# Pieces of one stage among the steps of the next: output projection and norm of a token segment between query chunks, a selection in two halves, a load two steps early

## The chip, the cores and the metric

The kernel runs on one core of a Trainium2 chip. The metric is device time in microseconds (us) of one execution, as the median over runs. TensorE (PE) multiplies, VectorE (DVE), ScalarE (ACT) and GpSimd (POOL) work on tiles, and SyncE (SP) issues most of the transfers; POOL issues the gathers. Each of them works through its own list of instructions in order.

## The reference, cut to what matters

One layer of a trunk: token mixers with carried states, their output projection, and a mixture of single-neuron experts that are found by product keys (`peer`). The part that the change touches begins where the mixers' branch outputs have been merged:

```python
out = jnp.einsum('bld,de->ble', merged, w_out)
h = h + out
xn = rms_norm(h, norm_ffn)
qh = jnp.einsum('td,de->te', xn, w_query).reshape(T, 8, 2, 128)
s = jnp.einsum('thpd,hpnd->thpn', qh, sub_keys)
sv, si = lax.top_k(s, 16)
cand = (sv[:, :, 0, :, None] + sv[:, :, 1, None, :]).reshape(T, 8, 256)
top_s, pos = lax.top_k(cand, 16)
gate = jax.nn.softmax(top_s, axis=-1)
act = jax.nn.gelu(jnp.einsum('thkd,td->thk', expert_u[eidx], xn))
y = jnp.einsum('thk,thkd->td', gate * act, expert_v[eidx])
```

Here T is 576 tokens, D is 1024 (8 blocks of 128), there are 8 heads with two half queries each, and eidx are the indices of the 16 chosen experts.

## The kernel before, in words

Products are taken in split precision: an operand becomes a high and a low part (`split`, L131: ACT writes the high part by a copy, DVE or POOL the low part by a subtraction in L134), and three matmuls (high·high, high·low, low·high) replace one (`mm3`, L136). Names ending in h and l are such parts. The weights of a block come in by `weights` (L142): SP loads the raw block of 512 KB into one of three buffers (`wraw`), the split puts its parts into one of two buffer pairs (`whl`).

The tokens stand in two segments, `SEG`: the first done is the one with 320 columns (called the first segment below), then the one with 256 (the second). The stages around the change are these.

- `merge` (L937) merges the branches, then for each segment does the output projection in 8 chunks e: 24 matmuls into `po`, and y = x + po on DVE (L974). After a segment's 8 chunks comes its RMS norm (`norm`, L980): the squares are summed (ACT squares, POOL adds, PE sums over partitions into `rmsrow`), turned and broadcast by small matmuls (`rmscol`, `rmsbc`), DVE computes the reciprocal root (L160 to L164), then eight times xnt = y·gain·rms (L986), and its two parts: x2gh and x2gl for the first segment, x2h and x2l for the second. For the first segment there are also transposes (`xtp`) that later stages read.
- `scored` (L1059) takes the queries, again segment by segment, in 16 chunks c (head and half). A chunk has 24 matmuls into `pq`, from the weight w_q[c], a copy to `qT` on ACT, and the scores `psc` against the keys on PE, one chunk later. ACT copies the scores to `sc`, and DVE finds the top 16 of each row block (`top16`, L1044: MAX8, FIND_INDEX8, MATCH_REPLACE8, MAX8, FIND_INDEX8). Chunks of heads 0 to 3 have two row blocks in the first segment, those of heads 4 to 7 have three. A chunk of the second segment has two.
- In the first segment the low part of w_q[c] is computed, by DVE for the first four chunks and by POOL for the other twelve, and written to DRAM (`wqd`); in the second segment it is loaded from there (L1041), in the chunk that uses it, while the high part is again a copy by ACT.
- After the first segment `select` (L1152) does the selection of the token block 0 for all 8 heads: candidates, top 16 of them (`tv`, `ti`), ranks, and the sums with `eq` that turn ranks into expert indices (`gi`). The gathers of expert rows, on POOL (L1379), need gi.
- After the second segment follows the long stage with all experts (`hidden`: `uh` and `ul` are parts of the expert weights in_u, `pz` its products).

A scheduler sets the order of the instructions of each engine from the program and its own estimates; the order of the buffers ("wr", "wl", "uh" and the like) follows the program. Three lines that say how the weights rotate:

```python
raw = self.wraw.tile([P, n, P], F32, name="wr", tag="wr")          # 3 buffers, w_out and w_q alike
hi = self.whl.tile([P, n, P], F32R, name="wh", tag="wh")           # 2 buffers
self.split(wh, wl, t, nc.vector if c < 4 else nc.gpsimd)           # first segment
```

Of the kernel before, what the change touches and what calls it, by code (L numbers as in the profile page):

```python
# [9 lines left out]
F32 = mybir.dt.float32  # L10
# [12 lines left out]
P = 128  # L23
D = 1024
# [97 lines left out]
class Net:  # L122
# [801 lines left out]
    def branches(self):  # L924

        nc = self.nc
        op = self.right.enter_context(self.pool("oT", side="right"))
        self.o = oh, ol = [], []
        for c in range(KC):
            t = op.tile([P, NT], F32, name="oraw", tag="ld", bufs=4)  # L930
            nc.sync.dma_start(t, self.spo[c // H][:, c % H, NMETA:])
            oh.append(op.tile([P, NT], F32R, name=f"oh{c}"))
            ol.append(op.tile([P, NT], F32R, name=f"ol{c}"))
            self.split(oh[c], ol[c], t)


    def merge(self):  # L937

        tc, nc, I = self.tc, self.nc, self.I
        oh, ol = self.o  # L940
        with self.pool("mg") as mp, self.pool("mw", 2) as wp, \
                self.pool("mps", 4, space=PSUM) as ps, self.pool("mps2", 1, space=PSUM) as ps2, self.pool("mps3", 1, space=PSUM) as ps3:
            mh = [mp.tile([P, NT], F32R, name=f"mh{c}") for c in range(KC)]
            ml = [mp.tile([P, NT], F32R, name=f"ml{c}") for c in range(KC)]
            for d in range(KC):
                wh, wl = self.weights(I["w_br"][d])
                sg = []
                for g in range(2):
                    t = wp.tile([P, NT], F32, name=f"sg{g}", tag=f"sg{g}")
                    nc.sync.dma_start(t, self.spl[8 + 2 * g + d // H][:, d % H, NMETA:])  # L950
                    sg.append(t)
                for o, w in SEG:
                    pa = [ps.tile([P, 512], F32, name="pbr", tag="ps") for _ in range(2)]
                    for g in range(2):
                        for k in range(H):
                            self.mm3(pa[g][:, :w], wh[:, H * g + k, :], wl[:, H * g + k, :], oh[H * g + k][:, o:o + w],
                                     ol[H * g + k][:, o:o + w], k == 0, k == H - 1)
                    for g in range(2):
                        v = sg[g][:, o:o + w]
                        nc.vector.tensor_tensor(v, v, pa[g][:, :w], op=ALU.mult)  # L960
                nc.vector.tensor_add(sg[0], sg[0], sg[1])
                self.split(mh[d], ml[d], sg[0])
# [789 lines left out]
```

## Time and profile before

| what | value |
|---|---|
| median of three runs | 1930.38 us (1926.36, 1930.38, 1931.58) |
| the profiled execution's own time | 1928.89 us |
| its span | 1927.1 us |
| PE busy | 1883.9 us, 98% |
| DVE busy | 1580.1 us, 82% |
| ACT, POOL busy | 908.3 us, 705.5 us |
| output projection of the second segment | about 618 to 648 us |
| query chunks, first and second segment | about 649 to 723 us, 723 to 781 us |

Between the span and the execution's own time lie 1.8 us. The page lists busy time by engine, the chain of work that ended last, and groups of instructions; the trace can also be asked for stretches, for waits of one engine (with the instruction that ended the wait), and for a timeline. A busy PE is one that has instructions under way, also where their pace is slow. The place of a time in this document is its distance from the start of the span.

### The profile page before, as it was taken

The numbers are of one execution on the slowest core, as the hardware profiler recorded it, in microseconds if no ns is written. First come the engines' busy times: TensorE is split into PE (matmuls) and PEld (weight loads), VectorE is DVE, ScalarE is ACT, GpSimd is POOL, SyncE is SP. The second block draws the span as 40 slices with busy tenths as digits, with TensorE's granted clock in tenths as the row PEclk, the third lists the DMA queues.
The fourth block names the chain that finished last, engine by engine and source line by source line (L and its number), as shares of the span: only waits on it lengthen the run. The fifth ranks groups of instructions, "written<-read, shape, count | busy, mean of one in ns | idle before, by whom it ended". The sixth has DMA issues, their size and how long they took to land.

```text
span 1927.1 us, 31932 instructions
## 1 busy us (share of the span) xinstructions
PE 1883.9 (98%) x11759; PEld 1715.2 (89%) x11759; DVE 1580.1 (82%) x2962; ACT 908.3 (47%) x1598; POOL 705.5 (37%) x519
## 2 busy tenths in 40 slices
PE   7999999999999999999999999999999999999998
PEld 7898999888999899999999999999888788787786
DVE  5677676676465779999999998788999888988897
ACT  5542334263324555544868899533333333333333
POOL 1110010300001241244444444466667565655660
PEclk9999999999999999999999999999999999999999
DMA  7355333465554879899999999999999999999993
GB/s 253 98 162 167 96 94 108 143 191 177 186 156 155 260 268 336 292 342 336 349 353 351 394 389 388 376 385 393 402 399 401 398 400 401 400 400 401 398 401 128
DMA packets 224388, 564.86 MB, mean 293 GB/s; under 512 B 31986, under 2 KB 96242, under 8 KB 222568
## 3 DMA queue, kind: packets, MB, share of 16 engines
q1 hardware_dynamic: 168792, 361.47, 53.0%
q0 software_dynamic: 55296, 201.35, 27.2%
q8 instruction: 92, 1.51, 0.3%
q14 instruction: 64, 0.52, 0.1%
q10 hardware_dynamic: 144, 0.01, 0.0%
HBM read 483.28 MB, written 78.16 MB: 291 GB/s over the span
## 4 chain that ended last, share of the span: by engine, by line
PE 65%; DMA 20%; DVE 12%; issue 2%; ACT 1%; SPq 0%; DVEq 0%; ACTq 0%
PE pz L138 9%; PE pz L140 9%; PE pz L139 8%; PE py L1591 7%; DMA wj<-wd 7%; PE acc L138 5%; PE acc L140 5%; PE acc L139 5%; DMA wr<-in_v 4%; DMA gz<-gz 4%; PE pw L1309 2%; DVE ul L1485 2%; PE py L666 1%; PE pz L661 1%; DVE gr L1391 1%
## 5 line engine op out<-in xcount | busy, mean ns | idle before, releaser
L1379 POOL DMA_INDIRECT gr<-in_ur,gi x192 | 300.9, 1567 | 321.0 <-DVE yt L1398 206.2
L1379 POOL DMA_INDIRECT gr<-in_v,gi x192 | 303.1, 1579 | 233.9 <-DVE gr L1391 172.1
L1479 ACT ACTIVATE uh<-wr 128x1024 fp32r<-128x1024 f32 x256 | 270.0, 1056 | 204.8 <-PE py L1591 95.7
L138 PE MATMUL pz<-x2h,uh 128*128 128x384 f32 x1024 | 346.6, 338 | 0.0
L140 PE MATMUL pz<-x2h,ul 128*128 128x384 f32 x1024 | 342.7, 335 | 0.2
L139 PE MATMUL pz<-x2l,uh 128*128 128x384 f32 x1024 | 342.3, 334 | 0.0
L1485 DVE TENSOR_TENSOR ul<-wr,uh 128x1024 fp32r<-128x1024 f32 x256 | 311.9, 1218 | 9.4 <-PE pz L140 3.9
L1398 DVE SCALAR_TENSOR_TENSOR yt<-gr,ga,yt 128x1024 f32<-128x1024 f32 x192 | 245.7, 1280 | 10.0 <-DMA gr<-in_v,gi 9.1
L1391 DVE SCALAR_TENSOR_TENSOR gr<-gr,xt 128x1024 f32<-128x1024 f32 x192 | 233.6, 1218 | 12.6 <-DMA gr<-in_ur,gi 12.4
L138 PE MATMUL acc<-xnh,wh 128*128 128x296 f32 (+1 forms) x768 | 233.1, 304 | 8.1 <-ACT xnh L299 6.5
L140 PE MATMUL acc<-xnh,wl 128*128 128x296 f32 (+1 forms) x768 | 233.5, 305 | 0.2 <-DVE wl L134 0.2
L139 PE MATMUL acc<-xnl,wh 128*128 128x296 f32 (+1 forms) x768 | 233.1, 304 | 0.5 <-DVE xnl L300 0.5
L1591 PE MATMUL py<-ul,ah 128*128 128x512 f32 x768 | 201.5, 396 | 4.7 <-DVE ul L1485 4.7
L1591 PE MATMUL py<-uh,ah 128*128 128x512 f32 x768 | 201.8, 397 | 3.3 <-ACT ah L1565 2.7
L1591 PE MATMUL py<-uh,al 128*128 128x512 f32 x768 | 200.6, 395 | 0.0
L140 PEld LDWEIGHTS pz<-x2h,ul 128*128 128x128 f32 x1024 | 192.2, 188 | 0.9 <-DVE ul L1485 0.9
L138 PEld LDWEIGHTS pz<-x2h,uh 128*128 128x128 f32 x1024 | 192.3, 188 | 0.1
L139 PEld LDWEIGHTS pz<-x2l,uh 128*128 128x128 f32 x1024 | 192.4, 188 | 0.0
L133 ACT ACTIVATE wh<-wr 128x1024 fp32r<-128x1024 f32 x88 | 93.1, 1058 | 197.5 <-issue 69.0
L1591 PEld LDWEIGHTS py<-ul,ah 128*128 128x128 f32 x768 | 143.3, 188 | 42.4 <-DVE ul L1485 8.2
L1591 PEld LDWEIGHTS py<-uh,ah 128*128 128x128 f32 x768 | 143.1, 188 | 39.2 <-ACT ah L1565 4.6
L1591 PEld LDWEIGHTS py<-uh,al 128*128 128x128 f32 x768 | 144.1, 188 | 35.1
(430 smaller groups left out, 3373.3 us busy)
## 6 DMA issues: line engine op xcount, KB each, us to landing
wr<-in_u SPq DMA_DIRECT2D x128, 512.0 KB, 6.9
wr<-in_v SPq DMA_DIRECT2D x128, 512.0 KB, 13.1
gz<-gz SPq DMA_DIRECT2D x96, 384.0 KB, 10.6
wr<-in_w_in SPq DMA_DIRECT2D x48, 512.0 KB, 3.7
wd<-wst SPq DMA_DIRECT2D x12, 2048.0 KB, 10.1
wj<-wd SPq DMA_DIRECT2D x96, 256.0 KB, 16.0
wr<-in_w_q SPq DMA_DIRECT2D x32, 512.0 KB, 5.1
wr<-in_w_out SPq DMA_DIRECT2D x16, 512.0 KB, 4.2
```

The costliest lines, as they stand in the source:

```text
L133: self.last_hi = self.nc.scalar.activation(hi, src, AF.Copy)
L138: mm(out, wh, xh, start=start, stop=False)
L139: mm(out, wh, xl, start=False, stop=False)
L140: self.last_mm = mm(out, wl, xh, start=False, stop=stop)
L661: mm(pz[:n, h, :n], U[:n, h, :n], X[:n, h, :n], start=True, stop=True)
L1309: nc.tensor.matmul(pw[:, u, :], oh[0][:, t], oh[2 + x][:, t], start=x == 0, stop=x == 1)
L1379: nc.gpsimd.indirect_dma_start(out=t, out_offset=None, in_=src, in_offset=bass.IndirectOffsetOnAxis(ap=self.gi[z][:, x, c:c + 1], axis=0))
L1391: nc.vector.scalar_tensor_tensor(t, t, 1.0, xt, op0=ALU.mult, op1=ALU.mult, accum_out=ga[:, c:c + 1])
L1398: nc.vector.scalar_tensor_tensor(yt, t, ga[:, c:c + 1], yt, op0=ALU.mult, op1=ALU.add)
L1479: self.nc.scalar.activation(w, self.raws[s], AF.Copy)
L1485: self.nc.vector.tensor_sub(w, self.raws.pop(s), self.ws[s][0].bitcast(F32))
L1591: nc.tensor.matmul(py[b][:, c, :], a[:, b * P:(b + 1) * P], w[:, 4 * c:4 * c + 4, :], start=start, stop=stop)
```

## The change

1. **Second segment's output projection and norm.** They leave `merge`, which now does the first segment alone. A generator `rest` holds them. Its chunks e = 0 and 1 stand ahead of the first segment's query chunks, e = 2 to 7 ahead of the chunks c = 6 to 11. The sum over partitions stands at c = 12, the broadcast and the first four of the eight blocks at c = 13, the other four at c = 14. The merged values of this segment lie in the buffers of `uh`, the y, squares and normed values in four of the five buffers of the gathers (`gr`). The five sums of squares that POOL did are done by DVE.
2. **First selection by halves.** `half(0)` does heads 0 to 3 in chunk 8 of the first segment, `half(HB)` heads 4 to 7 after its last chunk.
3. **Lower query weights two chunks ahead.** In the second segment the load of chunk c + 2's low part is issued in chunk c. Odd chunks have it in the buffers of `ul`, even ones in those of `wl`.

```diff
     def branches(self):
...
+        self.up = self.right.enter_context(self.pool("uw", 4, side="right"))
...
     def merge(self):
...
+            m1 = [[mp.tile([P, w1], F32R, name=f"m{x}{c}") for c in range(KC)] for x in "hl"]
+            m0 = [[self.up.tile([P, 4, w0], F32R, name="uh", tag="uh") for _ in range(KC // 4)] for x in "hl"]
...
-            for o, w in SEG:
-                for e in range(KC):
-                    x = wp.tile([P, NT], F32, name="xr", tag="ld")
-                    nc.sync.dma_start(x[:, :w], I["xT"][:, e, NMETA + o:NMETA + o + w])
-                    po = ps.tile([P, 512], F32, name="po", tag="ps")
-                    wh, wl = self.weights(I["w_out"][e])
-                    for k in range(KC):
-                        self.mm3(po[:, :w], wh[:, k, :], wl[:, k, :], mh[k][:, o:o + w], ml[k][:, o:o + w], k == 0, k == KC - 1)
-                    nc.vector.tensor_tensor(self.y[e][:, o:o + w], x[:, :w], po[:, :w], op=ALU.add)
-                self.norm(o, w, "norm_ffn", self.ffn_sink(o, w, ps3, wp), ps2, ps2, wp)
+            for e in range(KC):
+                x = wp.tile([P, w1], F32, name="xr", tag="ld")
+                nc.sync.dma_start(x, I["xT"][:, e, NMETA + o1:NMETA + o1 + w1])
+                po = ps.tile([P, 512], F32, name="po", tag="ps")
+                self.out_chunk(e, po[:, :w1], m1)
+                nc.vector.tensor_tensor(self.y[e], x, po[:, :w1], op=ALU.add)
+            self.norm(o1, w1, "norm_ffn", self.ffn_sink(o1, w1, ps3, wp), ps2, ps2, wp)
...
+    def rest(self):
+
+
+        nc, I = self.nc, self.I
+        o, w = SEG[1]
+        y = [self.gp.tile([P, 4, w], F32, name="gr", tag="gr") for _ in range(2)]
+        y = [y[k // 4][:, k % 4, :] for k in range(KC)]
+        sq, xs = (self.gp.tile([P, 4, w], F32, name="gr", tag="gr") for _ in range(2))
+        total = sq[:, 0, :]
+        n = KC - 3
+        for e in range(KC):
+            x = xs[:, e % 2, :]
+            nc.sync.dma_start(x, I["xT"][:, e, NMETA + o:NMETA + o + w])
+            po = self.pz.tile([P, 512], F32, name="po", tag="acc")
+            self.out_chunk(e, po[:, :w], self.m0)
+            nc.vector.tensor_tensor(y[e], x, po[:, :w], op=ALU.add)
+            nc.sync.dma_start(self.yd[:, e, o:o + w], y[e])
+            q = sq[:, 1 + e % 2, :] if e else total
+            if e > n:
+                nc.tensor.matmul(row[:, :w], self.c("ones")[:, :1], pq if e > n + 1 else total, start=e == n + 1, stop=False)
+            pq = q
+            nc.scalar.activation(q, y[e], AF.Square)
+            if 0 < e <= n:
+                nc.vector.tensor_add(total, total, q)
+            if e == n:
+                row = self.ps.tile([1, 512], F32, name="rmsrow", tag="ps")
+            yield
+        nc.tensor.matmul(row[:, :w], self.c("ones")[:, :1], pq, start=False, stop=True)
+        col, t = (self.ps.tile([P, 512], F32, name=n, tag="ps") for n in ("rmscol", "rmsbc"))
+        rw = self.np.tile([1, w], F32, name="rmsrw")
+        nc.vector.tensor_copy(rw, row[:, :w])
...
+        r = self.np.tile([P, nb], F32, name="rmsr")
+        nc.vector.tensor_scalar(r, col[:, :nb], 1.0 / D, EPS, op0=ALU.mult, op1=ALU.add)
+        self.rsqrt(r, self.np)
+        yield
...
+        for k in range(KC):
+            v = (sq[:, 3, :], xs[:, 2, :])[k % 2]
+            nc.vector.scalar_tensor_tensor(v, y[k], self.p("norm_ffn")[:, k:k + 1], t[:, :w], op0=ALU.mult, op1=ALU.mult)
+            self.split(self.x2h[k][:, o:o + w], self.x2l[k][:, o:o + w], v)
+            if k == KC // 2 - 1:
+                yield
...
+        def lower(c):
+            t = self.los[c] = (self.up if c % 2 else self.whl).tile([P, KC, P], F32R, name="wl", **(dict(tag="ul", bufs=3) if c % 2 else dict(tag="wl")))
+            nc.sync.dma_start(t.bitcast(F32), self.wqd[c])
...
             if not first:
                 nc.sync.dma_start(self.wqd[2 * PH - 1], self.wql.bitcast(F32))
+                lower(0)
+                lower(1)
...
             nc.scalar.activation(wh, t, AF.Copy)
-            nc.sync.dma_start(wl.bitcast(F32), self.wqd[c])
+            if c < 2 * PH - 2:
+                lower(c + 2)
+            wl = self.los.pop(c)
...
+            rest = self.rest()
+            for _ in range(2):
+                next(rest)
...
+                def half(h0):
+                    picked.append(self.select(0, self.gp, h0))
+                    while next(picked[-1]):
+                        pass
...
                 for c in range(2 * PH):
+                    if o + w == NT and c > 5:
+                        next(rest, None)
...
+                    if o and c == PH:
+                        half(0)
...
                 if o + w == NT:
-                    picked = self.select(0, self.gp)
-                    while next(picked):
-                        pass
+                    half(HB)
```

How the order moves. On PE, the first norm step of the second segment (`rmsrow`: sum over partitions). Before, it stood right behind the last `po` of the segment, ahead of the first query chunk:

```order
3456 L138 MATMUL po<-mh_5616,wh 128x256
3457 L139 MATMUL po<-ml_5624,wh 128x256
3458 L140 MATMUL po<-mh_5616,wl 128x256
3459 L190 MATMUL rmsrow<-rmssum,cst_66 1x256
3460 L190 MATMUL rmsrow<-rmssq,cst_66 1x256
3461 L1121 MATMUL pq<-x2gh_5578,wh 128x320
3462 L1122 MATMUL pq<-x2gl_5586,wh 128x320
3463 L1121 MATMUL pq<-x2gh_5579,wh 128x320
3464 L1122 MATMUL pq<-x2gl_5587,wh 128x320
3465 L190 MATMUL rmsrow<-rmssq,cst_66 1x256
```

Now, with `psc` the scores of the first segment's chunk 10, it stands in that segment's chunk 12:

```order
3769 L1165 MATMUL psc<-keys,qT 128x128 x2
3770 L1167 MATMUL psc<-keys,qT 128x128
3771 L1196 MATMUL pq<-x2gh_5585,wh 128x320
3772 L1197 MATMUL pq<-x2gl_5593,wh 128x320
3773 L1017 MATMUL rmsrow<-gr,cst_66 1x256
3774 L1196 MATMUL pq<-x2gh_5586,wh 128x320
3775 L1197 MATMUL pq<-x2gl_5594,wh 128x320
3776 L1196 MATMUL pq<-x2gh_5587,wh 128x320
3777 L1197 MATMUL pq<-x2gl_5595,wh 128x320
3778 L1196 MATMUL pq<-x2gh_5588,wh 128x320
3779 L1023 MATMUL rmscol<-cst_66,rmsrw 128x1 x2
3780 L1197 MATMUL pq<-x2gl_5596,wh 128x320
```

The row sum, the turned row and all that hangs on them moved behind eleven chunks' scores.

On DVE, the normed blocks of the second segment. Before, xnt and x2l stood behind each other, with a query weight's low part between them, and no top 16 had begun:

```order
762 L986 SCALAR_TENSOR_TENSOR xnt<-y_6181,par_67,rmsbc 128x256
763 L986 SCALAR_TENSOR_TENSOR xnt<-y_6182,par_67,rmsbc 128x256
764 L134 TENSOR_TENSOR wl<-wr,wh 128x1024
765 L134 TENSOR_TENSOR x2l_5567<-xnt,x2h_5559 128x256
766 L134 TENSOR_TENSOR x2l_5568<-xnt,x2h_5560 128x256
767 L986 SCALAR_TENSOR_TENSOR xnt<-y_6183,par_67,rmsbc 128x256
768 L986 SCALAR_TENSOR_TENSOR xnt<-y_6184,par_67,rmsbc 128x256
769 L134 TENSOR_TENSOR x2l_5569<-xnt,x2h_5561 128x256
770 L986 SCALAR_TENSOR_TENSOR xnt<-y_6185,par_67,rmsbc 128x256
771 L134 TENSOR_TENSOR x2l_5570<-xnt,x2h_5562 128x256
```

Now the same blocks (gr holds y and the normed values) stand among the top 16 of chunks 11 and 12:

```order
950 L1034 SCALAR_TENSOR_TENSOR gr<-gr,par_67,rmsbc 128x256
951 L1119 MAX sv<-mr 128x8
952 L1034 SCALAR_TENSOR_TENSOR gr<-gr,par_67,rmsbc 128x256
953 L1121 MAX_INDEX si<-sv,mr 128x8
954 L134 TENSOR_TENSOR x2l_5574<-gr,x2h_5566 128x256
955 L1113 MAX sv<-sc 128x8
956 L134 TENSOR_TENSOR x2l_5575<-gr,x2h_5567 128x256
957 L1034 SCALAR_TENSOR_TENSOR gr<-gr,par_67,rmsbc 128x256 x2
958 L1115 MAX_INDEX si<-sv,sc 128x8
959 L134 TENSOR_TENSOR x2l_5576<-gr,x2h_5568 128x256
960 L1117 MATCH_REPLACE mr<-sv,sc 128x128
961 L1113 MAX sv<-sc 128x8
```

Each block now waits its turn among MAX, MAX_INDEX and MATCH_REPLACE; the last of the eight x2l stands inside chunk 13's top 16.

## Rows read from the trace of the kernel before

**Rows 1.** The page, busy time of each engine over the span

```profile
PE 1883.9 (98%) x11759; PEld 1715.2 (89%) x11759; DVE 1580.1 (82%) x2962; ACT 908.3 (47%) x1598; POOL 705.5 (37%) x519
```

**Rows 2.** Busy time by stretch (start:end, length, each engine, PEclk, DMA share, GB/s)

```profile
650.00:700.00 50.00, 47.20 (x321) 46.22 (x321) 35.64 (x173) 24.05 (x58) 19.27 (x8) 0.97 0.76 260
...
900.00:1000.00 100.00, 99.92 (x680) 97.78 (x679) 99.28 (x186) 72.13 (x159) 47.58 (x29) 1.00 0.93 348
```

**Rows 3.** Waits of PE between 600 and 800 us: total, times, longest

```profile
PE pq L1124 <- DMA wl<-wqd: 3.5, 2, 1.9
PE psc L1097 <- ACT qT L1126: 3.0, 2, 2.5
PE psc L1097 <- DVE xnt L986: 2.8, 1, 2.8
```

**Rows 4.** Timeline of PE around 663 us: start, duration, instruction, [idle before]

```profile
663.02 0.31 PE L1121 MATMUL pq<-x2gh,wh 128*128 128x320 f32 x1
663.16 0.31 PE L1122 MATMUL pq<-x2gl,wh 128*128 128x320 f32 x1
666.27 0.71 PE L1097 MATMUL psc<-keys,qT 128*128 128x128 f32 x4 [2.79 <-DVE xnt L986]
...
668.95 0.47 PE L1121 MATMUL pq<-x2gh,wh 128*128 128x320 f32 x1
669.22 0.47 PE L1122 MATMUL pq<-x2gl,wh 128*128 128x320 f32 x1
```

**Rows 5.** Timeline of DVE, the second norm's x2l (x2 is two in a row), same columns

```profile
660.33 0.76 DVE L134 TENSOR_TENSOR x2l<-xnt,x2h 128x256 fp32r<-128x256 f32 x2 [1.42 <-ACT x2h L133]
...
662.92 2.90 DVE L134 TENSOR_TENSOR x2l<-xnt,x2h 128x256 fp32r<-128x256 f32 x2
```

**Rows 6.** Timeline of POOL at the same place

```profile
663.06 2.48 POOL L134 TENSOR_TENSOR wl<-wr,wh 128x1024 fp32r<-128x1024 f32 x1 [17.55 <-DVE wl L134]
```

**Rows 7.** Timeline of ACT at the end of the query stage

```profile
782.24 1.06 ACT L1479 ACTIVATE uh<-wr 128x1024 fp32r<-128x1024 f32 x1 [4.18 <-DMA wr<-in_u]
```

**Rows 8.** Timeline of DVE, last x2gl of the first norm

```profile
634.72 0.88 DVE L134 TENSOR_TENSOR x2gl<-xnt,x2gh 128x320 fp32r<-128x320 f32 x2
```

**Rows 9.** Timeline of PE: out-projection pairs, one query chunk, start of the second segment

```profile
647.80 0.28 PE L138 MATMUL po<-mh,wh 128*128 128x256 f32 x1
647.92 0.28 PE L139 MATMUL po<-ml,wh 128*128 128x256 f32 x1
...
692.24 0.60 PE L1097 MATMUL psc<-keys,qT 128*128 128x128 f32 x4
...
696.42 0.60 PE L1097 MATMUL psc<-keys,qT 128*128 128x128 f32 x4
...
723.05 0.36 PE L1121 MATMUL pq<-x2h,wh 128*128 128x256 f32 x1
```

**Rows 10.** Busy time, first segment's later chunks

```profile
678.40:723.00 44.60, 44.57 (x321) 44.38 (x321) 34.15 (x216) 24.33 (x55) 21.59 (x9) 1.00 0.79 267
```

**Rows 11.** Groups of DVE, 678.4 to 723 us: busy, mean ns, idle

```profile
L1057 DVE FIND_INDEX8 si<-sv,mr 128x8 uint32<-128x128 f32 x28 | 8.0, 286 | 0.0
```

**Rows 12.** Timeline of DVE, the first selection: its first, middle and last part

```profile
729.34 0.29 DVE L1161 CAST sb<-si 128x256 bf16<-128x256 uint32 x1
...
741.08 1.21 DVE L1210 TENSOR_TENSOR eq<-ra,io 128x2048 bf16<-128x2048 bf16 x1
...
750.97 0.47 DVE L1224 SCALAR_TENSOR_TENSOR gi<-ix,ix 128x128 int32<-128x128 bf16 x2
```

**Rows 13.** Groups of DVE, 615 to 668 us

```profile
L134 DVE TENSOR_TENSOR wl<-wr,wh 128x1024 fp32r<-128x1024 f32 x11 | 13.4, 1222 | 3.9 <-ACT wh L133 3.9
L986 DVE SCALAR_TENSOR_TENSOR xnt<-y,par,rmsbc 128x320 f32<-128x320 f32 (+1 forms) x16 | 7.5, 508 | 2.8 <-PE rmsbc L218 2.8
L134 DVE TENSOR_TENSOR x2l<-xnt,x2h 128x256 fp32r<-128x256 f32 x8 | 5.3, 687 | 2.0 <-ACT x2h L133 1.9
```

**Rows 14.** Groups of POOL, 668 to 725 us

```profile
L134 POOL TENSOR_TENSOR wl<-wr,wh 128x1024 fp32r<-128x1024 f32 x11 | 26.4, 2399 | 23.9 <-PE pq L1124 22.1 <-DMA wr<-in_w_q 1.8
```

More of the change, by code (lines that the diff above doesn't have):

```diff
@@ L926, in branches @@
         nc = self.nc
-        op = self.right.enter_context(self.pool("oT", side="right"))
+        self.up = self.right.enter_context(self.pool("uw", 4, side="right"))
+        self.ot = ExitStack()
+        op = self.ot.enter_context(self.pool("oT", side="right"))
         self.o = oh, ol = [], []
[L929 to L934, printed above, removed]
+        with self.pool("oraw", 4, side="right") as rp:
+            for c in range(KC):
+                t = rp.tile([P, NT], F32, name="oraw", tag="ld")
+                nc.sync.dma_start(t, self.spo[c // H][:, c % H, NMETA:])
+                oh.append(op.tile([P, NT], F32R, name=f"oh{c}"))
+                ol.append(op.tile([P, NT], F32R, name=f"ol{c}"))
+                self.split(oh[c], ol[c], t)
     def merge(self):
@@ new lines, in merge @@
+            self.ot.close()
+            wp = late.enter_context(self.pool("mx", 2))
+            self.y = [wp.tile([P, w1], F32, name=f"y{k}", bufs=1) for k in range(KC)]
+            for e in range(KC):
[4 more added lines that the diff above has]
+                nc.vector.tensor_tensor(self.y[e], x, po[:, :w1], op=ALU.add)
@@ new lines, in merge, with out_chunk @@
+            self.norm(o1, w1, "norm_ffn", self.ffn_sink(o1, w1, ps3, wp), ps2, ps2, wp)
+            for k in range(KC):
+                nc.sync.dma_start(self.yd[:, k, o1:], self.y[k][:, :MD - o1])
+    def out_chunk(self, e, po, m):
+        wh, wl = self.weights(self.I["w_out"][e])
+        for k in range(KC):
+            self.mm3(po, wh[:, k, :], wl[:, k, :], m[0][k], m[1][k], k == 0, k == KC - 1)
+    def rest(self):
[27 more added lines that the diff above has]
+        nc.vector.tensor_copy(rw, row[:, :w])
+        nb = w // P
+        for b in range(nb):
+            nc.tensor.matmul(col[:, b:b + 1], rw[:, b * P:(b + 1) * P], self.c("ones")[:1, :1], start=True, stop=True,
+                             skip_group_check=True)
+        r = self.np.tile([P, nb], F32, name="rmsr")
+        nc.vector.tensor_scalar(r, col[:, :nb], 1.0 / D, EPS, op0=ALU.mult, op1=ALU.add)
+        self.rsqrt(r, self.np)
+        yield
+        for b in range(nb):
+            self.after(nc.tensor.matmul(t[:, b * P:(b + 1) * P], r[:, b:b + 1].to_broadcast([P, P]), self.c("ident"), start=True, stop=True),
+                       self.last_mm)
+        for k in range(KC):
+            v = (sq[:, 3, :], xs[:, 2, :])[k % 2]
[3 more added lines that the diff above has]
+                yield
@@ L1066, in scored @@
         self.psu, self.tmp = ExitStack(), ExitStack()
-        self.up, self.gp, self.zp = (self.right.enter_context(self.pool(n, b, side="right")) for n, b in (("uw", 4), ("gat", 5), ("gzp", 3)))
+        self.gp, self.zp = (self.right.enter_context(self.pool(n, b, side="right")) for n, b in (("gat", 5), ("gzp", 3)))
         self.pz, self.ps = (self.psu.enter_context(self.pool(n, b, space=PSUM)) for n, b in (("acc", 3), ("rps", 5)))
```

122 lines of the change are left out of this document (60 added, 62 removed).

## The prediction

> **What bounds the kernel now.** The page comes first: PE is busy 1883.9 of 1927.1 us [rows 1]. All its idle time is 43 us, so no edit that leaves the matmuls alone can bring more, and the changed kernel issues as many. The question is which of these gaps lie in the stages that are edited, and what the new order puts there.
>
> Busy time by stretch comes second. Between 650 and 700 us DVE is busy 35.64 of 50 us: it has room, and PE lost 2.8 us and some clock (0.97). From 900 to 1000 us DVE is busy 99.28 of 100 and PE 99.92 [rows 2]: there both are full. Room on DVE exists early in this part of the program, not late.
>
> The waits of PE come third. Between 600 and 800 us three kinds are worth naming: 3.5 us for the lower query weights from DRAM, 3.0 us for qT, 2.8 us for a normed block [rows 3]. These 9.3 us are what the edits aim at.
>
> The timelines say what stands behind two of them. At 663.16 PE stops; the scores start at 666.27, and afterwards matmuls of 320 columns start 0.27 us apart where they stood 0.14 apart before [rows 4]. That is TensorE's lower clock level, behind 2.8 us without work. Of a query chunk of 24 matmuls it reached about 15, which cost some 2 us more: 4.7 us in all. The cause is on DVE. Two x2l took 2.90 us where another two took 0.76 [rows 5]; they ended when POOL's wl, started at 663.06, had run for 2.48 us [rows 6]. ACT stood behind them, and with it qT. The wait at the end of the queries is ACT's: uh waited 4.18 us for a load of in_u, and the next qT stood behind it [rows 7].
>
> **Part 1: projection and norm among the query chunks.** It removes the stall at 663 us, since no block of the second norm is computed there any more: -4.7 us. It also takes 144 of 192 `po` matmuls away from behind the first segment's norm, whose last x2gl is done at 635.6 [rows 8]. What is left there is 48 `po` at 0.12 us [rows 9], or 5.8 of the 23 that 192 gave, the transposes, and the first matmuls of two query chunks. Bounds: nothing (all of it still covered) and 5 us. I take 1, since PE already ran slower than its pace there before, and the first two query chunks are interleaved block by block.
>
> What it adds is not on PE but on DVE, and this is the main term. I follow DVE's new order from the scores of chunk 7 to the last x2l, which the first query chunk of the second segment needs in its 16th matmul.
>
> PE's side: seven query chunks of 4.18 us (692.24 to 696.42) are 29.3; three `po` chunks of 24 x 0.12 are 8.6 [rows 9]; the norm's small matmuls some 2; the matmuls ahead of the one that needs the last x2l another 2. Together **42 us**.
>
> DVE's side, in the same stretch:
> - Top 16: two sets of chunk 7, fifteen of chunks 8 to 12, 1.4 of chunk 13, so 18.4. The price of one set is 34.15 us of DVE [rows 10] by 28 sets [rows 11], 1.22 us. That is 22.4.
> - Half of the selection. Before, the whole lies between 729.34 and 751.4 us [rows 12], with about three top 16 sets among it, so 18 us. Half is 9 if all were proportional; the instructions have a fixed part, so I take 12.
> - Two wl of 1.22, and eight normed blocks of about 0.5 + 0.4 (the 687 ns of x2l in the group holds the disturbed one) [rows 5, 13]: 2.4 and 7.2, less some 0.08 for each of 16, as successive instructions overlap.
> - Three y and a total of squares, as wide as an x2l: 1.6. The reciprocal root and the copy of the row: some 2, an estimate.
>
> The sum is **46 us** (44 to 48). Three things come on top. The copy of the scores ahead of the first set takes 0.5. PE and DVE wait for each other at `rmsrow`, `rmscol`, `rmsbc` and at two wl: 0 to 4, I take 2. And POOL computes six wl of 2.40 us in this stretch [rows 14]. Rows 5 and 6 price one meeting with an instruction of DVE that reads two operands from SBUF: 2.1 us. The moved instructions (eq, totals, normed blocks, DVE's wl) are of that kind; before, they met almost none, because the selection came after the last of POOL's wl. MAX8 and its kin have one operand and kept their pace beside POOL: the 28 sets ran while POOL was busy 21.59 us [rows 10]. Bounds: 0 and 6 x 2.4 = 14.4; I take the middle, 7, since a two-operand instruction stands in every second or third place of this order.
>
> So the last x2l comes 0.5 + 46 + 7 + 2 = 55.5 us after the scores, and PE is there after 42: **+13.5 us**. It appears in pieces, at chunks 10 and 11 (total and wl of `po` e = 6 and 7), at `rmsbc`, and at 723 us. Behind a waiting matmul stand all later ones, the scores that DVE itself needs among them.
>
> The Trainium skill has a rule for this, in "SBUF: State Buffer", section "SBUF: two separate sides": the port pair that DVE and GpSimd share is an exclusive lock, held for a whole instruction, and a DVE operation with two SBUF inputs stands still against a GpSimd operation that reads SBUF. The x2l of rows 5 and POOL's wl of rows 6 agree with it (2.90 against 0.76 us). By the rule every such meeting waits out the rest of the wl, and the total would go toward the upper bound of 14.4 where I count 7.
>
> DVE's queue behind x2l holds the rest of chunk 13, chunks 14 and 15 and the second half of the selection. Nobody on PE waits for these soon (12 buffers of scores), and the second segment's chunks give DVE time again. I cost it at nothing.
>
> **Part 2: halves.** No more work but some fixed parts of instructions. It is counted above: it brings 12 us of DVE ahead of the x2l that stood behind them all.
>
> **Part 3: lower weights two chunks ahead.** The loads that PE waited for 3.5 us get more than 6 us of lead: -3.5 us. One row more on SP stands behind each; SP's transfers of w_out now also stand among the chunk's w_q loads in three raw buffers, so a `po` chunk's weights come later after POOL's wl than before. Bounds 0 and 6 x 1.5; I take nothing, as PE waits for DVE in those chunks anyway.
>
> The wait of 3.0 us at the end I leave as it is (bounds -3 and +4): uh still stands ahead of qT on ACT, now of two of them.
>
> **Sum.** -4.7 + 1 + 13.5 - 3.5 = +6.3 us. On the profiled execution's 1928.89 us that is 1935.2; its median stands 1.5 higher, 1930.38, so the forecast is **1936.7 us**.
>
> **Rivals.** 0.3% is 5.8 us, about what a measurement can tell from no change.
> - *DVE keeps up.* The place is the last x2l, the point is 2 us of delay or less. It needs the half selection at its lower bound (9 us), no mutual waits and a port that costs nearly nothing: 0.5 + 43 + 0.5 - 42 = 2. Then -4.7 + 0 + 2 - 3.5 = -6.2, or -9.2 if the end's qT comes on time too: **1921 to 1924 us**. For it: the scheduler's order leaves no obvious hole on PE. Against: 46 us of DVE on 42 of PE before any port. Chance 0.2.
> - *It cancels.* Delay of 4 to 12 us: -3 to +5, about **1931.5**. For it: the term's bounds are wide. Chance 0.27.
> - *The port costs its ceiling.* Each of six wl catches a two-operand instruction early: +7.4 on the forecast, **1944**. For it: rows 5. Against: MAX8 between them takes part of the meetings. Chance 0.12.
> - *ACT and the raw buffers.* uh waits for in_u ahead of two qT, or w_out arrives late for `po`, and the clock falls behind a stall: +3 to +8 more, **1940 to 1945**. Chance 0.06.
> - *Not what it says*: the lower weights are late all the same, because SP is held by buffers: +3.5, **1940**. Chance 0.03.
>
> The forecast's own case (delay 12 to 17 us, +5 to +9) keeps 0.32. Its share above 5.8 us and the last three make slower 0.43; cancelling and the lower share of the forecast make no difference 0.37; faster 0.2. The range takes in 1922 (half of the first rival) to 1946 (the ceiling).
>
> **What the profile will show.** Right: no wait at 663 us for xnt and none for wl from DRAM; DVE above 95% from the scores of chunk 7 on; waits of PE for DVE at `po` e = 6 and 7, at `rmsrow` or `rmsbc`, and at the first x2l, 11 to 16 us together; two-operand instructions of DVE of 1 to 2.5 us while POOL's wl runs. Wrong: PE over 98% busy there, or the second segment's queries beginning before 722 us, which would be the first rival; waits for `wr` from w_out, the fourth.

## The result, and the profile after

The changed kernel is slower: its median is 1939.42 us (1928.94 to 1940.64) beside 1928.99 us (1922.92 to 1935.32) for the kernel before in the same comparison. The ratio is 1.0058 [1.0039, 1.0078], or some 11 us, twice the 0.3% that a measurement can tell. Forecast were +6.3 us and "slower" as the likeliest sign; the measured median lies in the range.

The time is laid out by three marks on PE that exist in every kernel here: the first matmul of the merge (`pbr`), the first and the last query matmul of the second segment, and the last product `pz` of the long stage. All figures come from one profile each. Kernels that differ only behind the queries repeat the first row to 0.03 us in two pairs (196.39 and 196.38; 183.00 and 183.03) and differ by 1.3 us in a third (191.22 and 192.54); a difference of that size is not read here.

| us | before | after | difference | forecast |
|---|---|---|---|---|
| first `pbr` to first query matmul of the second segment | 186.85 | 196.39 | +9.54 | +9.8 |
| from there to the last query matmul | 57.18 | 54.75 | -2.43 | -3.5 |
| from there to the last `pz` | 585.26 | 588.93 | +3.67 | 0 |

The three rows add up to +10.8 us; the two profiled executions differ by 8.3 us (1937.24 and 1928.89), since what lies ahead of these marks and behind them took 2.4 us less in the second. So most of the loss stands where it was forecast. Whether it stands there for the forecast's reason is the question of the experiments.

The page first, against [rows 1]: PE's busy time is 4 us longer with as many instructions. That points to work at a lower pace, not to more work.

```profile
PE 1887.7 (98%) x11759; PEld 1718.6 (89%) x11759; DVE 1589.8 (82%) x3008; ACT 911.6 (47%) x1611; POOL 689.7 (36%) x514
```

Second, busy time by stretch (columns as in [rows 2]). The last line is the stretch for which the prediction made its sum, from the scores of chunk 7 to the last x2l.

```profile
650.00:700.00 50.00, 43.99 (x311) 41.92 (x310) 39.67 (x176) 23.73 (x49) 13.53 (x6) 0.97 0.69 236
690.00:700.00 10.00, 7.66 (x47) 7.26 (x47) 10.00 (x43) 3.52 (x7) 2.09 (x2) 0.85 0.48 166
700.00:710.00 10.00, 8.16 (x37) 6.63 (x37) 6.84 (x34) 1.32 (x2) 1.02 (x1) 0.67 0.49 163
710.00:720.00 10.00, 9.42 (x61) 8.33 (x60) 6.02 (x33) 5.96 (x13) 7.10 (x3) 0.96 0.47 170
675.30:735.30 60.00, 50.57 (x324) 46.15 (x323) 52.39 (x245) 29.42 (x63) 19.44 (x10) 0.91 0.65 223
```

PE idles here: it is busy for 43.99 of 50 us from 650, before for 47.20 [rows 2], and for 50.57 of 60 in the stretch of the sum, where a large part of the same place had 44.57 of 44.60 [rows 10]. Then look at DVE: it is full from 690 to 700 us and idle for 7.1 of the next 20 us, while PE goes on losing time. If DVE alone were the bound it would not idle there. The granted clock falls to 0.67 behind the stalls, between full speed and the lower level (1.2 of 2.4 GHz); over the 30 us from 690 that is 0.15 + 0.33 + 0.04 of 10 us each, 5.2 us of work at full speed.

Third, PE's waits between 600 and 850 us, against [rows 3] (the five largest):

```profile
PE psc L1165 <- ACT qT L1201: 4.6, 1, 4.6
PE po L140 <- DVE wl L134: 2.5, 3, 1.8
PE rmsrow L1009 <- DVE gr L1013: 2.3, 1, 2.3
PE po L138 <- ACT wh L133: 1.3, 1, 1.3
PE psc L1165 <- ACT qT L1203: 1.3, 1, 1.3
```

The two waits that the change aimed at, for xnt at 663 us and for wl from DRAM, are gone. New ones for DVE and ACT have come among the `po` chunks, and the largest is at the end of the query stage.

Fourth, DVE's timeline beside POOL's, against [rows 5, 6]. DVE:

```profile
679.36 0.21 DVE L1238 CAST sb<-si 128x128 bf16<-128x128 uint32 x1
...
679.88 0.38 DVE L1246 TENSOR_TENSOR cand<-sv 128x224 f32<-128x224 f32 x1
680.19 2.38 DVE L1249 TENSOR_TENSOR cand<-sv 128x32 f32<-128x32 f32 x1
...
688.40 2.39 DVE L1269 CAST rb<-ti 128x64 bf16<-128x64 uint32 x1
...
698.40 0.18 DVE L1296 TENSOR_TENSOR ix<-eq 128x64 bf16<-128x64 bf16 x1
...
698.83 2.41 DVE L1302 SCALAR_TENSOR_TENSOR gi<-ix,ix 128x64 int32<-128x64 bf16 x2
```

And POOL:

```profile
654.46 2.40 POOL L134 TENSOR_TENSOR wl<-wr,wh 128x1024 fp32r<-128x1024 f32 x1 [7.01 <-ACT sc L1168]
662.99 2.41 POOL L134 TENSOR_TENSOR wl<-wr,wh 128x1024 fp32r<-128x1024 f32 x1 [6.14 <-DMA wqd<-wl]
671.54 2.41 POOL L134 TENSOR_TENSOR wl<-wr,wh 128x1024 fp32r<-128x1024 f32 x1 [6.13 <-DMA yd<-gr]
680.05 2.46 POOL L134 TENSOR_TENSOR wl<-wr,wh 128x1024 fp32r<-128x1024 f32 x1 [6.11 <-DMA yd<-gr]
688.23 2.51 POOL L134 TENSOR_TENSOR wl<-wr,wh 128x1024 fp32r<-128x1024 f32 x1 [5.72 <-DMA yd<-gr]
```

Three instructions of 0.2 us or so (of the two gi, the first) took 2.3 to 2.4 us each beside a wl (the gi beside the one that POOL began at 698.65); with smaller meetings at 718 and 724 us that is 7.1 to 7.7 us. And POOL's wl, one per chunk, stand 8.2 to 8.6 us apart here, with POOL idle between them. A chunk with an output-projection piece needs 4.18 + 24 x 0.12 = 7.06 us of PE. Something other than PE's pace holds POOL.

Fifth, the chain of waits says what (start, us, piece):

```profile
645.05 2.41 POOL wl L134
647.85 6.44 DMA wqd<-wl
654.46 2.40 POOL wl L134
...
660.26 5.98 DMA wr<-in_w_out
666.35 1.07 ACT wh L133
667.44 1.23 DVE wl L134
```

A query weight's low part is written to DRAM, 6.44 us; only then does POOL begin the next one. `whl` has two buffer pairs, and weights of w_out and w_q now alternate in them, so each stream has one: POOL's next wl must wait until the store of its last one has read the buffer. Where POOL's rows above name the store of y (`yd`), the same wl waits for this store too: the store of the wl ahead was issued 5.3 to 5.7 us before each of the last four starts, and y lies in other buffers. The raw loads behind it on SP need buffers that POOL's wl must first have read, so w_out's block comes late too.

Last, the end of the query stage, ACT's timeline, against [rows 7]:

```profile
780.70 0.37 ACT L1201 ACTIVATE qT<-pq 128x256 f32<-128x256 f32 x1
...
789.52 1.06 ACT L1557 ACTIVATE uh<-wr 128x1024 fp32r<-128x1024 f32 x1 [7.23 <-DMA wr<-in_u]
790.48 0.37 ACT L1201 ACTIVATE qT<-pq 128x256 f32<-128x256 f32 x1
```

uh waits 7.23 us where it waited 4.18, and PE's clock falls behind its wait for qT: 790 to 800 us after, then before.

```profile
790.00:800.00 10.00, 9.10 (x41) 9.10 (x42) 9.40 (x53) 5.74 (x10) 0.00 (x0) 0.70 0.65 260
...
790.00:800.00 10.00, 10.00 (x59) 9.84 (x58) 9.83 (x47) 4.64 (x6) 1.87 (x2) 1.00 0.60 195
```

The chain there runs through DVE:

```profile
783.81 1.12 DVE ul L1563
784.93 0.39 DVE sv L1113 x2
...
787.34 1.21 DVE ul L1563
...
790.48 0.38 ACT qT L1201
790.90 1.22 PE psc L1165 x4
```

The load behind uh is issued at 784.96, when DVE's first ul has ended and let go of a raw buffer.

### The profile page after: what moved, and what is told of

It reads as the page before. It is cut to its first block, busy times and chain, and to the rows that moved or that the text cites. A ratio compares the mean times of both kernels' runs of the same rounds, so it can differ in the third digit from the quotient of the medians.

```text
span 1935.5 us, 31985 instructions
## 1 busy us (share of the span) xinstructions
PE 1887.7 (98%) x11759; PEld 1718.6 (89%) x11759; DVE 1589.8 (82%) x3008; ACT 911.6 (47%) x1611; POOL 689.7 (36%) x514
## 4 chain that ended last, share of the span: by engine, by line
PE 67%; DMA 20%; DVE 10%; issue 2%; ACT 1%; POOL 0%; SPq 0%; DVEq 0%; POOLq 0%; ACTq 0%
PE pz L138 9%; PE py L1669 9%; PE pz L140 9%; PE pz L139 9%; DMA wr<-in_v 8%; DMA gz<-gz 5%; PE acc L138 4%; PE acc L140 4%; PE acc L139 4%; DMA wj<-wd 4%; PE pw L1387 2%; PE py L666 1%; PE pz L661 1%; PE pbr L138 1%; PE pbr L140 1%
## 5 line engine op out<-in xcount | busy, mean ns | idle before, releaser
L1457 POOL DMA_INDIRECT gr<-in_v,gi x192 | 297.8, 1551 | 250.8 <-DVE gr L1469 185.5
```

The lines of the kernel that those rows point to most:

```text
L1457: nc.gpsimd.indirect_dma_start(out=t, out_offset=None, in_=src, in_offset=bass.IndirectOffsetOnAxis(ap=self.gi[z][:, x, c:c + 1], axis=0))
```

## The experiments

My theory behind the prediction was that DVE alone sets the pace of the moved pieces. The rival that the profile after raises is the ring of two buffer pairs (the **ring** below). Ratios are to the kernel before, run on the same chip in the same comparison; their intervals span 2 to 4 us to either side, so two experiments whose intervals overlap are not ranked by time. "Start" is the table's first row (before 186.85, after 196.39).

**The first selection behind the loop.** From the changed kernel; both halves stand behind the query chunks.

```diff
-                    if o and c == PH:
-                        half(0)
...
+                    half(0)
                     half(HB)
```

> The changed kernel, but the first selection stands whole behind the first segment's query chunks, as in the kernel before. Theory A (DVE's work ahead of the last x2l sets PE's delay): 12 us of DVE leave that stretch, and with them two of the four long meetings with POOL's wl (4 us); PE's waits for DVE at rmsrow, wl of po 7, rmsbc and the first x2l (2.4 + 2.1 + 0.9 + 1.4 us in the profile of the changed kernel) fall below 2 us together, the lower clock behind them goes, and the second segment's queries begin 6 to 10 us earlier. The end of the queries stays late (3 to 5 us). Whole: 6 to 10 us faster than the changed kernel, so at or a little below the kernel before. Theory B (the ring of weight buffers: POOL's wl, the store of it, the next wl, then SP's loads of w_out into three raw buffers, with 8.5 us for each chunk where PE needs 7.7): the scores stay 8.5 us apart and less than 3 us is won.

Measured: 1932.61 us, 1.0033 [1.0019, 1.0047], start 191.73. Some 5 us of the loss are gone, between what the two theories said, but it tells less than it seems to: the scheduler still put instructions of the first half among the chunks, since heads 0 to 3 were ready. The largest wait was 5.5 us, `rmscol` for DVE. DVE's selection was thinned, not taken out.

**The third uh behind the last qT.** From the changed kernel.

```diff
...
+                        else:
+                            self.after(self.last_uh, last_q)
...
```

> The changed kernel, with the third part uh on ACT held behind the last copy qT. In the profile of the changed kernel PE waited 4.6 us there for qT and then ran some 5 us at the lower clock level. Theory: ACT's order alone makes that wait; it goes, and 5 to 7 us are won against the changed kernel. Rival: the wait moves to the first products pz, which need the parts of in_u anyway, or DVE's lag takes its place: less than 2 us.

Measured: 1936.25 us, 1.0051 [1.0032, 1.0070], beside 1.0058. ACT's order was not the cause at the end: the wait of 4.6 us for qT went and one of 3.2 us for DVE's ul took its place at `pz`.

**Lower weights early, alone.** From the kernel before, part 3 of the change only (`lower`, as in the diff of the change).

> The kernel before with the third part of the change alone: lower query weights loaded two chunks ahead. Theory: the two waits of PE for these loads (3.5 us) go and nothing comes in their place: ratio 0.998 to the kernel before. Rival: the load competes with the others all the same, or PE's earlier arrival is spent in the wait for qT at the end: ratio 1.000.

Measured: 1927.70 us, 1.0017 [1.0004, 1.0029]. The wait for wl from DRAM is gone and nothing is gained. PE's waits from 600 to 850 us show what is late next:

```profile
PE psc L1106 <- ACT qT L1135: 3.2, 4, 1.9
PE pz L140 <- DVE ul L1494: 2.1, 2, 1.9
PE psc L1106 <- DVE xnt L986: 0.9, 1, 0.9
```

The stretch to the last query matmul was even longer (58.06 against 57.18 us), but in this profile the start is 183.42, 3.4 us shorter than before, though nothing of parts 1 and 2 is in it. At the stall of [rows 5, 6] POOL's wl began 0.56 us later, counted from the first `pbr`, and met one x2l instead of two:

```profile
665.88 2.56 POOL L134 TENSOR_TENSOR wl<-wr,wh 128x1024 fp32r<-128x1024 f32 x1 [18.18 <-ACT x2h L133]
...
667.09 1.63 DVE L134 TENSOR_TENSOR x2l<-xnt,x2h 128x256 fp32r<-128x256 f32 x1 [0.48 <-ACT x2h L133]
```

PE waited 0.9 us there and not 2.8. How many executions of the kernel before have the long stall, one profile can't say. The median doesn't show what this profile gains.

**Low parts of the query weights in buffers of their own.** From the changed kernel; those of the chunks 6 to 15 go to the three buffers of `ul`, which takes the ring away and leaves DVE its work.

```diff
-            wl = self.whl.tile([P, KC, P], F32R, name="wl", tag="wl")
+            wl = (self.up if c > 5 else self.whl).tile([P, KC, P], F32R, name="wl", **(dict(tag="ul", bufs=3) if c > 5 else dict(tag="wl")))
```

> The changed kernel, with the low parts of the first segment's chunks 6 to 15 in three buffers of their own, so that a chunk's wl need not wait for the store of the chunk before. Theory B (ring): POOL's wl comes 2 us earlier in each chunk, the scores stand 7.7 us apart up to chunk 8, the waits for wh go, 3 to 6 us are won. Theory A (DVE): the order before chunk 8 is smoother, but DVE is as late at rmsrow, wl and x2l: less than 2 us.

Measured: 1928.45 us, 1.0012 [0.9998, 1.0026], start 190.29. This one edit takes away 6.1 us of the start and most of the loss; its interval lies clear of the changed kernel's. POOL's timeline:

```profile
651.40 2.40 POOL L134 TENSOR_TENSOR wl<-wr,wh 128x1024 fp32r<-128x1024 f32 x1 [5.90 <-ACT wh L133]
658.46 2.39 POOL L134 TENSOR_TENSOR wl<-wr,wh 128x1024 fp32r<-128x1024 f32 x1 [4.67 <-ACT wh L133]
665.52 2.39 POOL L134 TENSOR_TENSOR wl<-wr,wh 128x1024 fp32r<-128x1024 f32 x1 [4.67 <-ACT wh L133]
```

They stand 7.06 us apart, PE's own pace, and wait for wh instead of a store (farther on, where DVE is behind, 6.3 to 11.4). The stretch of the sum, and the 30 us where DVE idled above:

```profile
672.40:727.10 54.70, 46.55 (x324) 43.83 (x323) 51.91 (x243) 28.95 (x62) 19.23 (x10) 0.97 0.71 231
...
690.00:720.00 30.00, 25.73 (x181) 23.86 (x180) 28.52 (x121) 15.06 (x32) 13.22 (x6) 1.00 0.65 212
```

Now DVE is busy for 95% of both, and the stretch takes 54.7 us where the prediction had 55.5. What is left after the ring is, in the main, what the prediction described.

**Both of these.** The edits of the first and of the last experiment together.

> The changed kernel with both causes taken away: the first selection whole behind the first segment, and low parts of chunks 6 to 15 in buffers of their own. In their profiles the first alone began the second segment's queries 4.7 us sooner after the start of the branch products than the changed kernel, the second alone 6.1 us. Theory (two causes that add): 9 to 11 us sooner, so at about the place of the kernel before or up to 2 us ahead of it; against the kernel before, ratio 0.997 to 1.000. Rival (one chain, in which the second cause only waits behind the first): 6 to 7 us sooner, ratio 1.001 to 1.002.

Measured: 1931.93 us, 1.0021 [1.0004, 1.0038], start 191.22: no better than the last one alone. As in the first, selection work had stayed among the chunks; PE waited 3.4 us at `rmscol`, 3.3 at `rmsrow`, 3.2 for a qT.

**POOL's last wl on DVE.** From the changed kernel, to try the meetings with POOL: no wl of POOL among chunks 10 to 15.

```diff
-            self.split(wh, wl, t, nc.vector if c < 4 else nc.gpsimd)
+            self.split(wh, wl, t, nc.vector if c < 4 or c > 9 else nc.gpsimd)
```

> The changed kernel, with the low parts of chunks 10 to 15 computed by DVE and not by POOL. DVE gets 6 x 1.14 = 7 us of work and loses the 7.7 us that its instructions stood behind POOL's wl in the profile of the changed kernel; the ring gets 1.2 us shorter per chunk, for chunks 10 and 11 above all. Theory (port and ring cost what the profile shows): even on DVE, 2 to 4 us won. Rival (DVE's queue is the limit and wl waits its turn there behind top 16): no gain, or up to 5 us slower.

Measured: 1933.44 us, 1.0040 [1.0022, 1.0058], start 191.80. The start is 4.6 us shorter, but the edit does two things: a wl on DVE can't meet one on POOL, and POOL's 2.4 us fall out of the chain through the ring. It can't separate them.

**Lower weights early, and chunk 4's wl on DVE.** From the kernel before: part 3, and POOL's first wl (the one of [rows 6]) given to DVE.

```diff
...
-            self.split(wh, wl, t, nc.vector if c < 4 else nc.gpsimd)
+            self.split(wh, wl, t, nc.vector if c < 5 else nc.gpsimd)
...
```

> The kernel before with the third part of the change, and with the low part of chunk 4 on DVE instead of POOL, so that no wl of POOL runs beside the second norm. Theory: the wait at 663 us (2.8 us and the lower clock behind it) came from the meeting of an x2l with POOL's wl; it goes without any move of the norm, 2 to 5 us faster than the third part alone. Rival: DVE's extra 1.2 us ahead of the last x2l keep qT late: no change.

Measured: 1926.42 us, 0.9999 [0.9984, 1.0015], start 183.63. Without a wl beside them all x2l took 0.42 us, and the start is 3.2 us shorter than before. It is no shorter than with part 3 alone (183.42), so the profiles don't show that this edit adds to it. At the end PE waited 4.8 us for ul: no change in time.

**ul off DVE.** The kernel with both edits, and the low parts of the first two expert weights on POOL.

```diff
-            self.nc.vector.tensor_sub(w, self.raws.pop(s), self.ws[s][0].bitcast(F32))
+            (self.nc.gpsimd if s < 2 else self.nc.vector).tensor_sub(w, self.raws.pop(s), self.ws[s][0].bitcast(F32))
```

> As the version with both causes taken away, and the low parts of the first two in_u blocks computed by POOL, which is idle at the end of the queries, while DVE works off its top 16. In the runs so far PE waited 2 to 5 us there, for qT behind uh or for ul behind top 16. Theory: the wait at the first products pz falls below 1 us and 2 to 4 us are won against the version with both. Rival: DVE's lag shows at the next ul, or POOL's slow subtraction (2.4 us) and its place behind the gathers take the gain: within 1 us.

Measured: 1930.76 us, 1.0019 [1.0001, 1.0036], beside 1.0021 without it. In its profile the part behind the last query matmul is 6.4 us shorter (583.80 against 590.21), but the medians differ by 1.2 us. The table's third row, from a single profile, is not to be trusted to a few us; I rest nothing on it alone.

**The selection truly behind the loop.** From the changed kernel: one undivided selection of all 8 heads, as before, so that it can't start early. The ring stays.

```diff
-                    if o and c == PH:
-                        half(0)
...
-                    half(HB)
+                    half(0)
...
-        n, H = P, HB if b == 1 or spare else PH
+        n, H = P, HB if b == 1 else PH
...
```

> The changed kernel with the first selection undivided, on all 8 heads as in the kernel before, so that it can't begin ahead of the last top 16. (Where it stood in two halves behind the loop, the first half still ran among the chunks: its ranks and eq stand between 688 and 705 us in the profile of the version with both causes taken away. That version did not take DVE's work out.) Theory A (DVE): 12 us of DVE and most of the 7 us behind POOL's wl leave the stretch; the waits at rmsrow, rmsbc, x2l go; the ring of buffers (8.5 us for a chunk) is left. The second segment's queries begin 186 to 190 us after the start of the branch products, where the changed kernel took 196.4 and the kernel before 186.9. Against the changed kernel 5 to 10 us faster. Theory B (ring alone): no more than the 4.7 us that the halves behind the loop brought.

Measured: 1935.47 us, 1.0039 [1.0022, 1.0056], start 190.14. The stretch of the sum:

```profile
673.60:727.20 53.60, 46.99 (x307) 43.14 (x306) 37.90 (x173) 23.81 (x55) 16.65 (x7) 0.93 0.67 231
```

DVE has 15.7 us to spare here, and the stretch is still 53.6 us long. POOL's wl stand 8.0 to 8.4 us apart, about as in the changed kernel. This is the ring without DVE's selection.

The start is 6.2 us shorter than the changed kernel's, yet the ratio is not clear of 1.0058, and 5 to 10 us were expected. The second segment's queries, beside which the selection now lies, take 60.75 us where they took 54.75: at the last query matmul only 0.2 of the 6.2 us are left.

**That, and buffers of their own.** The edits of the last experiment and of the fourth.

> The undivided selection, and low parts of chunks 6 to 15 in buffers of their own. Theory (DVE's work and the ring are the whole loss in this stretch): no wait above 1.5 us is left between the branch products and the second segment's queries, which begin 181 to 184 us after them, 3 to 6 us sooner than in the kernel before; the end of the queries then gives some of it back, since the selection lies there again: ratio 0.997 to 1.000 to the kernel before. Rival (a third cause, such as raw loads behind POOL's wl): a start at 186 or later, ratio above 1.001.

Measured: start 183.00, as expected; but 1931.56 us, 1.0024 [1.0007, 1.0042], where 0.997 to 1.000 was expected. The stretch:

```profile
675.00:721.40 46.40, 42.94 (x308) 40.53 (x308) 35.44 (x170) 23.85 (x54) 16.74 (x7) 1.00 0.79 269
```

With the ring and DVE's selection both away, the loss of the start is gone and 3.9 us are won on before. They are given back: 2.0 in the second segment's queries (59.17 us against 57.18), the rest behind them. PE's largest waits from 600 to 850 us, and DVE from 750 to 800 us:

```profile
PE pz L140 <- DVE ul L1562: 5.8, 1, 5.8
PE psc L1165 <- ACT qT L1201: 2.2, 2, 1.8
PE psc L1165 <- ACT qT L1203: 2.1, 1, 2.1
...
750.00:800.00 50.00, 42.04 (x304) 41.26 (x303) 49.90 (x297) 21.83 (x36) 7.27 (x8) 0.97 0.77 281
```

DVE is full; PE comes earlier to `pz` and waits there for ul.

**That, and the end freed.** To it, the low parts of the first two expert weights on POOL and the third uh behind the last qT.

> As the one before, with the low parts of the first two in_u blocks on POOL and the third uh on ACT held behind the last qT, the two edits at the end of the queries together. Theory: uh behind qT moved the wait to the first ul on DVE, and ul on POOL takes that away, so that PE waits below 1 us from the end of the queries to 800 us: 3 to 5 us faster than the version without, ratio 0.994 to 0.998 to the kernel before. Rival: whatever is won there is lost again behind it, as DVE's queue is full until 1000 us and the later stages are bound by PE and by transfers: within 1.5 us of the version without.

Measured: 1930.09 us, 1.0016 [1.0000, 1.0033]. The wait for ul fell to 3.2 us, that for qT rose to 4.0. A third ul on DVE still came late.

**The kernel before with the small parts.** From the kernel before: part 3, chunk 4's wl on DVE, the first two ul on POOL, the second and third uh behind the last qT. Nothing of parts 1 and 2.

```diff
...
-            self.split(wh, wl, t, nc.vector if c < 4 else nc.gpsimd)
+            self.split(wh, wl, t, nc.vector if c < 5 else nc.gpsimd)
...
+                        if s:
+                            self.after(self.last_uh, last_q)
...
-            self.nc.vector.tensor_sub(w, self.raws.pop(s), self.ws[s][0].bitcast(F32))
+            (self.nc.gpsimd if s < 2 else self.nc.vector).tensor_sub(w, self.raws.pop(s), self.ws[s][0].bitcast(F32))
```

> The kernel before with the third part of the change, chunk 4's low part on DVE, the low parts of the first two in_u blocks on POOL, and the second and third uh on ACT behind the last qT. The version without the last two edits waited 4.8 us for the first ul on DVE and 2 us for qT. Theory (DVE's queue, which is full from 700 us on, is what every order pays in the end, and 2 x 1.2 us of it leave): those waits shrink, 2 to 5 us faster than that version, ratio 0.997 to 0.999 to the kernel before. Rival: a later ul or POOL's gathers take the gain: ratio 0.9995 to 1.001.

Measured: 1924.58 us, 0.9980 [0.9961, 0.9998], the lowest ratio of the twelve, by an interval that ends just below 1; it is within the 0.3% that a measurement can tell. PE's largest waits:

```profile
PE pz L140 <- DVE ul L1496: 4.8, 1, 4.8
PE psc L1106 <- ACT qT L1135: 1.8, 2, 1.3
PE psc L1106 <- DVE xnt L986: 0.4, 1, 0.4
```

## Why the prediction was right, and where it was not

The sign and the place were right, and so was the sum up to the second segment's queries: -4.7 + 1 + 13.5 = +9.8 forecast, +9.54 measured. That agreement is luck: one part of the 13.5 was too large, and a cost taken at nothing made up for it. Four kernels, with and without each cause, take it apart:

| | ring there | ring away |
|---|---|---|
| selection halved, among the chunks | 196.39 | 190.29 |
| selection undivided, behind the loop | 190.14 | 183.00 |

- **The stall gone, less cover: -4.7 + 1 = -3.7.** With both causes away the start is 183.00 - 186.85 = -3.85 us. The size agrees. That moving the norm is what brought it isn't shown: with part 3 alone the start was 183.42.
- **DVE's side, 46 us of work and 7 of the port.** In the stretch of the sum DVE was busy 52.4 us in the changed kernel and 51.9 without the ring: right to about a microsecond, and so is the port's 7 (7.1 to 7.7 measured). Only part of the port's meetings were with instructions of two operands, as the text assumed; one was a CAST.
- **PE's side, 42 us.** Its work was right (42.94 us busy in the kernel without either cause), but the stretch took 46.4 there, since PE keeps waits there that are not DVE's selection: 1.2 us for `rmsr` and 2.1 for qT. So DVE's lag with the selection among the chunks is worth not 13.5 but 54.7 - 46.4 = 8.3 us of the stretch, or 7.3 of the start (190.29 - 183.00).
- **The step that failed: "I take nothing, as PE waits for DVE in those chunks anyway".** This was said of the weights that come later behind POOL's wl, with bounds of 0 and 9 us. The ring costs 7.1 us by itself (190.14 - 183.00), and 6.1 on top of DVE's work (196.39 - 190.29). The two add up almost in full (13.4 of 14.4 us). Why, is argued: with the ring DVE and PE wait by turns, and DVE's 7.1 us of idle time between 700 and 720 end with PE's `po`, PE's `rmsrow` and a root on ACT; without the ring DVE idles 1.5 us of the 30 from 690. I had named the three raw buffers and overlooked that two pairs of `whl`, shared by alternating streams, leave each weight one pair, with a store to DRAM in the cycle. The term of 13.5 came out right because what DVE lacked the ring supplied.
- **These prices hold for the start.** Counted to the last query matmul, the four kernels of the table take 251.14 and 244.97 us in the first line, 250.89 and 242.17 in the second. The ring still costs 6.2 and 8.7 us; the selection among the chunks costs 0.2 and 2.8, since elsewhere it makes the second segment's queries longer.
- **The lower clock** was counted in a rival only. It is part of the above: 0.91 over the stretch in the changed kernel, 0.93 with the ring alone, 0.97 with DVE's work alone, 1.00 with neither. Times the length of each stretch that is 5.4, 3.8, 1.6 and 0 us at full speed, so about half of what the ring costs is the clock.
- **Part 3, -3.5.** The two waits went, and the part from the first to the last query matmul shrank by 2.43 us. In the time it is worth nothing: alone it gave 1.0017.
- **The end, "I leave as it is".** The 3.0 us of [rows 3] held one wait of 0.5 at 733.7 us; the one at the end was 2.5 and grew to 4.6, with 0.70 of the clock behind it where it was 1.00. It is not ACT's order, as the prediction had it: DVE is busy 9.97 us of the 10 from 780, uh's load waits for a buffer that DVE's ul releases, and where uh was put behind qT, `pz` waited for ul. DVE's queue behind the last x2l, which the prediction cost "at nothing", shows here.

The next table follows five kernels past the queries: how far behind the kernel before (+) or ahead of it (-) each is, counted from the first `pbr`. The 151st `pz` comes some 30 us behind the last query matmul.

| us | first query matmul | last query matmul | 151st `pz` | last `pz` |
|---|---|---|---|---|
| the changed kernel | +9.5 | +7.1 | +11.5 | +10.8 |
| ring away | +3.4 | +0.9 | +1.5 | +2.5 |
| selection behind the loop | +3.3 | +6.9 | +11.9 | +11.2 |
| both away | -3.9 | -1.9 | +3.4 | +2.6 |
| before, with the small parts | -4.0 | -6.6 | -1.8 | -2.5 |

Four of the five lose 4.4 to 5.2 us in those 30 us: the changed kernel by its wait for qT, the last three by one wait for ul (4.8 to 5.8 us), and all four by the clock behind it. The 3.7 us of the third row lie there too, not in the long stage. What the last two had won ahead of that place is lost there, all of it or most.

Two of the prediction's signs did not come. DVE was not above 95% from the scores of chunk 7 on, but busy 52.39 of 60 us (87%); and PE's waits for DVE at `po`, `rmsrow` and `rmsbc` sum to 5.5 us, not 11 to 16. The rest of the delay is the lower clock and waits for ACT and POOL.

The rivals: the fourth, ACT and the raw buffers with the clock, was given 0.06 and came nearest in its mechanism; it was written as an addition to the forecast case, and about that is what happened. That DVE keeps up is refuted by the first table's column without the ring, where the selection among the chunks costs 7.3 us. Its sign, queries of the second segment before 722 us, didn't come: they began at 731.25.

By the Trainium skill ("SBUF: State Buffer", section "SBUF: two separate sides") every such meeting waits out the rest of the wl; the prediction took from it that the port's cost would go toward 14.4. The trace agrees with the lock (2.38 and 2.41 us for cand and gi), and the cost stayed at half, because MAX8 and its kin and operations with an operand in PSUM stood in the other places.

What stays open: what would be won if every late ul left DVE, which was not tried; how often the stall at 663 us stands in executions of the kernel before; and why part 3 alone, 3.2 us ahead at the last `pz` of its profile, is no faster by its median (1.0017).

## What to carry to other kernels

When a second stream is put among the steps of a first, write down for every rotating buffer how many each stream now has, and what must read a buffer before it comes free; a store counts. Before a gain is booked, look for the next place where the same engine needs the busiest one: here a wait taken away ahead of a full DVE came back there. And a sum that agrees with the measurement is not yet an explanation; the two causes here showed only when each was taken away without the other.

## What was not expected

A CAST with a single operand, uint32 to bf16 and 128x64, took 2.39 us beside POOL's wl, where a larger one with no wl beside it took 0.21 us. I had priced such meetings for two operands alone. The Trainium skill names casts among the operations that can take the shared port pair, in "SBUF: State Buffer", section "Who interferes with whom"; this trace agrees.

The scheduler pulled the first half of a selection into the chunks though the program had it behind them. Only the undivided selection, which needs all heads, took it out.
